# A conformer convolution on one core: output weights loaded ahead of their split, and the modulation's matmuls placed inside the channel tiles

## Chip, core and metric

The kernel runs on one core of one Trainium2 chip. The metric is the device time of one execution in microseconds (us). Before the change the median of three timed runs is 2841.52 us (2840.78 to 2841.62).

## The reference

Two layers run over 256 context tokens ("prompt", p) and 2048 latent tokens ("sample", s), of width 1024. Layer 0 is a convolution branch, layer 1 a neighbourhood attention. The change touches layer 0 alone:

```python
def conv_branch(h, w_in, dw_w, dw_b, ln_g, ln_b, w_out):
    a, b, z = jnp.split(h @ w_in, 3, axis=-1)
    u = a * jax.nn.sigmoid(b)
    u = lax.conv_general_dilated(u, dw_w[:, None, :], ...,        # 31 taps, one filter per channel
                                 feature_group_count=CONV_WIDTH) + dw_b
    u = layer_norm(u, ln_g, ln_b)
    u = jax.nn.silu(u) * jax.nn.silu(z)
    return u @ w_out
...
        shift, scale, gate = ada_params(c, ada_w[i], ada_b[i])    # silu(c) @ w + b, in three parts
        h = modulate(x, norm_g[i], shift, scale)
...
        x = x + gate[:, None] * out
```

## The kernel before

**Products.** Everything is float32. A weight or activation is split into a rounded high part and the rest (hi, lo), and a product is the sum of three matmuls: hi by hi, lo by hi, hi by lo (`project`, L351 to L353). A product of 128 channels by 512 tokens takes 8 x 3 = 24 matmuls of 128x512.

**Channel tiles.** `conv_layer` goes twice through eight channel tiles of 128 channels: first with the tokens of chunk A, then with chunk B, the two sample blocks of 512 tokens that begin at 1024 and 1536. Tiles are numbered 0 to 15 here, so tiles 8 to 15 are chunk B, and tile 15 is the last. A chunk B tile has six products, named (part, block): part 1 is the sigmoid's argument, part 0 is a, part 2 is z. The order is (1,0), (1,1), (0,0), (0,1), (2,0), (2,1), and in tile 8 (1,0), (0,0), (2,0), (1,1), (0,1), (2,1). All products of a tile, and the modulation's matmuls, take turns in two PSUM banks ("mm"), in the order in which they are issued. A bank is free when its product has been evacuated: part 1 by ACT (L449, sigmoid), part 0 by VectorE (L451, u = a * sigmoid, called the u evacuation), part 2 by ACT (L454, copy of z, which then goes to memory).

**The filter.** Each tile's 31-tap filter is cut into two halves of the token range, cv_n_0 and cv_n_1 (n is the channel tile). ACT makes scaled copies (L480) that GpSimd adds up (L483) for 11 or 12 of the taps. VectorE does the other taps as a chain of multiply-adds in two PSUM accumulators of the pool "acc" (L500, L502; L498 on ACT begins the second), and joins both sums (L506). Half 1 comes first on VectorE, then half 0, which begins from GpSimd's sum. Each tile's u evacuation (0,1) starts the chain on its own half 1. The result goes to memory (L510, `vc_d`).

**The modulation.** The vectors shift, scale and gate come from `ada_chunk`: a load of 2 MB of weights (adaw, L211), 16 matmuls of 32 output rows (ada, L216), a copy to SBUF on ACT (adam, L221), and then either a transposing matmul and an addition for a gate part (adat L225, adao L228, stored to memory L229 and read back as the `gate` rows L245) or eight small ones for shift and scale (adat L232, L239). Eight chunks are spread over the ends of tiles 8 to 15: two of layer 0's gate, six of layer 1.

**The layer norm.** `norm_stages` normalizes 128 tokens: load (L681, L683), reduction over channels (L687), mean by a matmul (L695), subtraction (L697), square (L700), variance (L706), scale as a diagonal (L709, L712) spread by a matmul (ln_rb, L715), multiplication (L719), eight Silu (L722), multiplication by silu(z) (L726), and the split of the result on GpSimd (L105, L108). Prompt tiles p0 and p128 and sample tile s0 run inside the convolution, in the buffer `ln_work`.

**The output weights.** `out_weight` loads w_out in eight pieces of 128x1024 into two buffers ("raw"), each followed by its split: co_h on ACT (L747) and co_l on VectorE (L111). The parts go into two "slot" buffers each for hi and lo, which had held other things: the first lo buffer holds the activations of block 1024, read by (2,0) of the last tile. `conv_out_pipeline` then multiplies: per 128 tokens two halves of 512 outputs, each in two quarters of 12 matmuls (co_p, co_s; L821, L822, L824), then the gate and the residual on VectorE (L830, L831).

**What sets the order.** In `conv_layer` each step is an event with a time, `at(t, f)`; the events are sorted by time, and that is the order of issue on TensorE, ACT, VectorE and GpSimd. The times are a plan in us; no instruction waits for them. The layer norm of s0, the gates and `out_weight` are written behind `conv_layer`. On VectorE, ACT and GpSimd the scheduler places them; `high_priority` moves a step as far ahead as its inputs and buffers are planned to allow. SP's loads and stores run in the queue's order, and one whose buffer is not free holds up those behind it. `conv_out_pipeline` has its own fixed order on TensorE. Its PSUM pool "lnps" lies where "acc" was, so its first layer-norm matmul (ln_s_mu of s128, L695) cannot start before VectorE's last join L506 of cv_7_0. The modulation's placing is these lines, with ADA_TIME = 3.1:

```python
        for j, (i, c) in enumerate([(0, 4), (0, 5)] + [(1, c) for c in range(6)]):
            g = self.ada_chunk(i, c)
            t = begin[NK + 1 + j] - ADA_TIME
            for dt in (-ADA_AHEAD, 0, 0.1, ADA_TIME - 0.5, ADA_TIME + ADA_LAG, ADA_TIME + ADA_LAG + 1.2)[: 6 if c < 4 else 5]:
                at(t + dt, step_of(g))
```

Of the kernel before, what the change touches and what calls it, by code (L numbers as in the profile page):

```python
# [11 lines left out]
F32 = mybir.dt.float32  # L12
# [6 lines left out]
P = 128  # L19
D = 1024  # L20
NK = D // P
# [18 lines left out]
ADA_TIME = 3.1  # L40
# [3 lines left out]
LN_TIMES = (0, 6, 14, 18, 21, 25, 33, 37, 47, 49, 52, 54, 54.1, 60, 62)  # L44
ADA_AHEAD = 4.0
ADA_LAG = 3.5
LEAD = 1.9
TMP = 4
BEGIN = 10
# [27 lines left out]
class Kern:  # L77
# [278 lines left out]
    def conv_layer(self, part_a, part_b):  # L356
# [4 lines left out]
        nc, io = self.nc, self.io  # L361
# [5 lines left out]
        begin, free = [0.0], [0.0, 0.0]  # L367
# [6 lines left out]
        for s in range(2 * NK):  # L374
# [32 lines left out]
            t = base  # L407
# [106 lines left out]
            def put(t, f, *args):  # L514
                at(t, lambda: f(*args))


            t = max(done[0], free[0])
            put(t - 0.2, scaled, 0, 0, ("sum", 0))
            for tap in range(1, npool):  # L520
                put(t + 0.6 - LEAD, scaled, 0, tap, (0, tap))
                put(t + 0.6, add, 0, tap)
                t += pool_step[0]
            ready = t + 0.8
            t = max(done[1], free[1])
# [5 lines left out]
            t = swap  # L531
# [6 lines left out]
            t = swap + 0.3  # L538
            for tap in range(npool - 1):
                put(t - LEAD, scaled, 1, tap, (1, tap))  # L540
                put(t, add, 1, tap)
# [81 lines left out]

        for j, (i, c) in enumerate([(0, 4), (0, 5)] + [(1, c) for c in range(6)]):
            g = self.ada_chunk(i, c)
            t = begin[NK + 1 + j] - ADA_TIME
            for dt in (-ADA_AHEAD, 0, 0.1, ADA_TIME - 0.5, ADA_TIME + ADA_LAG, ADA_TIME + ADA_LAG + 1.2)[: 6 if c < 4 else 5]:
                at(t + dt, step_of(g))

        for i, (load, rms, first, every, gap) in enumerate(((begin[3], begin[3] + 14, begin[3] + 26, 3.0, 30), (begin[7] + 3, begin[7] + 14, begin[8] - 7.6, 1.2, 9.6))):  # L630
            src, t0, n = part_b[i]
            for pair in range(2):
# [27 lines left out]
                t = first + gap * pair  # L660
# [75 lines left out]
            pass  # L736
        return y[0]

    def out_weight(self, w, name, res):

        nc = self.nc
        for k in range(NK):
            if k % 4 == 0:
                hi, lo = (self.slot(F32R, f"{name}_{s}{k}", [P, NK // 2, D]) for s in "hl")
            raw = self.raw(w[k * P : k * P + P, :], [P, D], f"{name}_raw{k}")
            yield
            nc.scalar.copy(hi[:, k % 4, :], raw)  # L747
            self.rest_dve(lo[:, k % 4, :], raw, hi[:, k % 4, :])
            res[0].append(hi[:, k % 4, :])
            res[1].append(lo[:, k % 4, :])  # L750
            yield

    def conv_out(self, w, blocks, ready, res=None):
# [511 lines left out]
    def phase1(self):  # L1265
        tc = self.tc
        with ExitStack() as c:
            late = c.enter_context(ExitStack())
            self.rp = late.enter_context(tc.tile_pool(name="rp", bufs=1, side="right"))
            self.sp = Tagged(c.enter_context(tc.tile_pool(name="sp", bufs=1)), {"slot": 4, "t4": 8, "raw": 2, "st": 6})  # L1270
            self.sm = c.enter_context(tc.tile_pool(name="sm", bufs=3))
            self.ps = c.enter_context(tc.tile_pool(name="ps", bufs=2, space=bass.MemoryType.PSUM))
            with tc.tile_pool(name="convp", bufs=2) as self.up, tc.tile_pool(name="acc", bufs=2, space=bass.MemoryType.PSUM) as self.pc:
                E = mybir.EngineType
                ordered = {E.PE, E.Activation, E.DVE, E.Pool}
                with tc.manual_schedule(engines=ordered):
                    self.conv_layer([("p", 0, 256), ("s", 0, 512), ("s", 512, 512)], [("s", 1024, 512), ("s", 1536, 512)])
                work = self.room[0]
                self.ready.append(self.conv_norm("s", 0, [work[:, i] for i in range(3)] + [self.t4(F32R, f"ln_s0_y{t}") for t in "hl"]))
                self.gate = [self.spread_row(self.t4(F32, f"gate0_{g}", [P, D]), self.gate_d[0, g]) for g in range(2)]  # L1280
                w = [[], []]
                for _ in self.out_weight(self.io["conv_w_out"][0], "co", w):
                    pass
            self.hp = c.enter_context(tc.tile_pool(name="hp", bufs=1))
            extra = c.enter_context(ExitStack())
            self.xp = extra.enter_context(tc.tile_pool(name="extra", bufs=1))
            norms = extra.enter_context(ExitStack())
            self.pc = norms.enter_context(tc.tile_pool(name="lnps", bufs=1, space=bass.MemoryType.PSUM))
            A, B = [], []
            rest = [("s", 768, 256), ("s", 1024, 512), ("s", 1536, 512)]  # L1290
            with tc.manual_schedule(engines={E.PE}):
                ready = self.conv_out_pipeline(w, [("p", 0, 256), ("s", 0, 512), ("s", 512, 256)], self.ready, [("s", 768), ("s", 896)], A)
            out = self.conv_out(w, rest, ready)
            self.weave(self.na_rest(A), out, 2)
            prep = itertools.chain(out, *(self.layer1_block(*b, B) for b in rest[1:]))
            self.weave(self.na_values(A, lambda: None), prep, 2)
            for _ in itertools.chain(prep, self.layer1_block(*rest[0], B)):
                pass
            late.close()
            norms.close()  # L1300
            rest = self.na_rest(B)
            with tc.tile_pool(name="bp", bufs=1, side="right") as self.bp:
                with tc.tile_pool(name="mb", bufs=1, side="right") as self.mb:
                    side = itertools.chain(self.context_keys(), self.masked_bias())
                    self.weave(self.na_values(B, lambda: next(rest)), side, 2)
                    self.weave(itertools.islice(rest, 13), side, 3.6)
                    for _ in side:
                        pass
                with tc.tile_pool(name="pq", bufs=2, side="right") as pq, tc.tile_pool(name="pqs", bufs=1, space=bass.MemoryType.PSUM) as pps:
                    side = itertools.chain(self.gated_weights(), self.context_values())  # L1310
                    side = self.mixed(self.prompt_attention(pq, pps), side, 40 / 52)
                    self.weave(itertools.islice(rest, 8), side, 11.5)
                    for _ in side:
                        pass
            extra.close()
            self.start_attention()
            for _ in rest:
                pass
# [435 lines left out]
```

## Time and profile before

| what | value |
|---|---|
| timed runs, median (least to greatest) | 2841.52 us (2840.78 to 2841.62) |
| the profiled execution, its own time | 2847.02 us |
| its span, from the first to the last instruction | 2845.2 us |
| granted TensorE clock, mean | 0.981 |
| busy in the span: TensorE, VectorE, ACT, GpSimd | 95%, 65%, 51%, 53% |
| the convolution's products of the last tile end at | 703.9 us |
| first layer-norm matmul of the output pipeline | 739.99 us |

In the profile PE is TensorE (PEld its weight loads), DVE VectorE, ACT ScalarE, POOL GpSimd, and SPq the queue of SyncE that issues the DMAs. A row of a timeline has its start and its length, then engine, line, operation, output<-input, tile and number of instructions; in brackets stands how long the engine was idle before it, and what released it. Names have lost their numbers: cv_s stands for the sums of all tiles.

### The profile page before, as it was taken

How to read it: one execution, taken by the hardware profiler on the slowest of the kernel's cores; microseconds unless marked ns; L12 is line 12 of the kernel's file. 1: busy time of each engine (PE TensorE's matmuls, PEld its weight loads, DVE VectorE, ACT ScalarE, POOL GpSimd, SP SyncE). 2: the span in 40 equal slices, each digit the busy share in tenths (PEclk: the TensorE clock that was granted, in tenths of full speed). 3: DMA queues.
4: the chain of work that ended last, by engine and by line, in shares of the span. 5: the costliest groups of instructions: out<-in, count | busy, mean ns of one | idle time of the engine just before them, and what ended most of it. 6: DMA issues, size and time to landing. Idle time of an engine off the chain costs nothing. (4 is left out here: it accounts for less than half of the span.)

```text
span 2845.2 us, 45399 instructions
## 1 busy us (share of the span) xinstructions
PE 2702.7 (95%) x16079; PEld 2339.1 (82%) x16079; DVE 1848.0 (65%) x3126; ACT 1448.6 (51%) x2544; POOL 1507.1 (53%) x1631
## 2 busy tenths in 40 slices
PE   6999999999899999999989999879999999999998
PEld 4888877777677888999988888768888898888887
DVE  4789989999886510023455632157787787777885
ACT  4457565667544311234222244246676666666774
POOL 4679878889653343355113325235555555455563
PEclk9999999999899999999999999999999999999999
DMA  7233554555445554447789996688876787866763
GB/s 254 68 121 117 185 187 158 179 177 187 154 120 164 165 156 130 131 141 229 240 285 347 346 307 194 185 247 221 245 206 190 200 216 181 239 184 178 199 168 105
DMA packets 435627, 548.02 MB, mean 193 GB/s; under 512 B 42945, under 2 KB 306201, under 8 KB 435272
## 3 DMA queue, kind: packets, MB, share of 16 engines
q1 hardware_dynamic: 430080, 522.17, 61.3%
q10 hardware_dynamic: 5320, 22.95, 2.1%
q8 instruction: 128, 2.10, 0.3%
q14 instruction: 99, 0.81, 0.1%
HBM read 359.86 MB, written 189.22 MB: 193 GB/s over the span
## 5 line engine op out<-in xcount | busy, mean ns | idle before, releaser
L1508 POOL TENSOR_SCALAR sa_p<-sa_p,sa_m 128x992 f32<-128x992 f32 (+2 forms) x256 | 278.6, 1088 | 445.7 <-DVE sa_m L1507 321.7
L502 DVE SCALAR_TENSOR_TENSOR cv<-u,dw,cv 128x640 f32<-128x640 f32 (+2 forms) x570 | 427.9, 822 | 3.7 <-ACT cv L498 2.8
L1523 ACT CAST sa_pt<-sa_T 128x512 fp32r<-128x512 f32 (+3 forms) x512 | 275.2, 588 | 235.0 <-PE sa_T L1514 230.6
L111 DVE TENSOR_TENSOR sa_pt<-sa_T,sa_pt 128x512 fp32r<-128x512 f32 (+3 forms) x512 | 328.4, 682 | 3.2 <-ACT sa_pt L1523 3.0
L351 PE MATMUL ci_ps<-h_s_hi,ci_wh 128*128 128x512 f32 x768 | 307.5, 400 | 2.0 <-DVE shift L239 1.0
L353 PE MATMUL ci_ps<-h_s_hi,ci_wl 128*128 128x512 f32 x768 | 303.2, 395 | 0.0
L352 PE MATMUL ci_ps<-h_s_lo,ci_wh 128*128 128x512 f32 x768 | 302.9, 394 | 0.0
L1500 DVE TENSOR_REDUCE sa_m<-sa_S 128x1 f32<-128x512 f32 x256 | 176.2, 688 | 184.2 <-PE sa_S L1482 169.7
L1506 ACT ACTIVATE sa_p<-sa_S,sa_m 128x992 f32<-128x992 f32 (+2 forms) x256 | 267.3, 1044 | 53.7 <-DVE sa_m L1502 42.4
L1514 PE MATMUL sa_T<-ident,sa_p 128*128 128x128 f32 (+3 forms) x2048 | 271.6, 275 | 8.1 <-DVE sa_pt L111 7.3
L1514 PEld LDWEIGHTS sa_T<-ident,sa_p 128*128 128x128 f32 (+3 forms) x2048 | 238.5, 138 | 42.5 <-issue 12.0
L480 ACT ACTIVATE cv_p<-u,dw 128x640 f32<-128x640 f32 (+2 forms) x326 | 241.4, 770 | 55.4 <-POOL cv_s L483 37.7
L483 POOL TENSOR_TENSOR cv_s<-cv_s,cv_p 128x519 f32<-128x519 f32 (+1 forms) x155 | 233.1, 1504 | 68.3 <-DVE cv_s L506 45.5
L483 POOL TENSOR_TENSOR cv_p<-cv_p,cv_p 128x520 f32<-128x520 f32 (+1 forms) x155 | 227.7, 1469 | 27.1 <-ACT cv_p L480 19.5
L1543 PE MATMUL sa_O<-sa_pt,a_v 120*128 120x256 f32 (+5 forms) x1280 | 192.5, 281 | 0.0
L1538 PE MATMUL sa_O<-sa_pt,cv 128*128 128x256 f32 x1024 | 176.3, 295 | 4.2 <-DVE 1_0_of L1557 1.7
L351 PEld LDWEIGHTS ci_ps<-h_s_hi,ci_wh 128*128 128x128 f32 x768 | 145.5, 189 | 39.3 <-ACT cv_p L480 2.5
L1502 DVE CUSTOM_DVE_ANT_0 sa_S<-sa_S,a_bm,sa_m 128x480 f32<-128x480 f32 (+2 forms) x256 | 170.9, 668 | 9.1
L353 PEld LDWEIGHTS ci_ps<-h_s_hi,ci_wl 128*128 128x128 f32 x768 | 145.1, 189 | 33.8
L352 PEld LDWEIGHTS ci_ps<-h_s_lo,ci_wh 128*128 128x128 f32 x768 | 145.6, 190 | 30.9
L1543 PEld LDWEIGHTS sa_O<-sa_pt,a_v 120*128 120x128 f32 (+2 forms) x1280 | 169.1, 193 | 0.0
L351 PE MATMUL ni_s<-h_s_hi,nis_wh 128*128 128x512 f32 x384 | 152.2, 396 | 12.4 <-DVE ni_s_l L111 8.7
(843 smaller groups left out, 7198.6 us busy)
## 6 DMA issues: line engine op xcount, KB each, us to landing
adaw<-in_ada_w SPq DMA_DIRECT2D x24, 1024.0 KB
ci_w<-in_conv_w_in SPq DMA_DIRECT2D x48, 512.0 KB
a_bm<-bm_d SPq DMA_DIRECT2D x32, 720.0 KB
x_s<-in_x_sample SPq DMA_DIRECT2D x32, 512.0 KB
vs_d<-v_s SPq DMA_DIRECT2D x128, 128.0 KB
a_qh<-qh_d SPq DMA_DIRECT2D x128, 128.0 KB
a_ql<-ql_d SPq DMA_DIRECT2D x128, 128.0 KB
o_x<-x_d SPq DMA_DIRECT2D x32, 512.0 KB
```

The lines of the kernel that those rows point to most:

```text
L111: self.nc.vector.tensor_tensor(out=lo, in0=src, in1=hi.bitcast(F32), op=ALU.subtract)
L351: self.nc.tensor.matmul(out, wh[:, k, :], hh[:, k, :], start=k == 0, stop=False)
L352: self.nc.tensor.matmul(out, wh[:, k, :], hl[:, k, :], start=False, stop=False)
L353: self.nc.tensor.matmul(out, wl[:, k, :], hh[:, k, :], start=False, stop=k == NK - 1)
L480: nc.scalar.activation(t, st["u"][:, c0 + tap : c1 + tap], AF.Copy, scale=self.dw[:, ct, tap : tap + 1])
L483: nc.gpsimd.tensor_tensor(out=st["sum", half], in0=st["sum", half], in1=st[half, tap], op=ALU.add)
L502: nc.vector.scalar_tensor_tensor(out=out, in0=u, scalar=w, in1=first, op0=ALU.mult, op1=ALU.add)
L1506: nc.scalar.activation(p[:, n], S[:, n], AF.Exp, scale=-1.0, bias=m[:, 2:3], accum_out=m[:, 3:4])
L1508: nc.gpsimd.tensor_scalar(out=p[:, n], in0=p[:, n], scalar1=m[:, 3:4], scalar2=1.0, op0=ALU.mult, op1=ALU.mult)
L1514: nc.tensor.transpose(t[:w, c * P : c * P + P], p[:, x + c * w : x + c * w + w], self.ident)
L1523: nc.scalar.copy(pt[:w, 0, part, :, at], t)
L1543: nc.tensor.matmul(dst, v[:w, c0 + c].rearrange("p s d -> p (s d)"), loc[:, lo:hi], start=False, stop=s == 1 and c == 3)
```

## The change

Two things change. Each of the modulation's eight chunks stands 12 us earlier in the table of events. And `out_weight` is started before the layer norm of s0 and the gates: it asks for seven pieces at once, 0, 1, 3 and 4 in buffers of the pool "t4", 2 in the unused fourth part of `ln_work`, 5 and 6 in "raw"; piece 7 is asked for after the split of piece 5. Both parts of the split have high priority.

```diff
+ADA_EARLY = 12.0
...
-            t = begin[NK + 1 + j] - ADA_TIME
+            t = begin[NK + 1 + j] - ADA_TIME - ADA_EARLY
...
-    def out_weight(self, w, name, res):
+    def out_weight(self, w, name, spare, res):
...
+        room = lambda k: self.t4(F32, f"{name}_raw{k}", [P, D]) if k in (0, 1, 3, 4) else self.sp.tile([P, D], F32, tag="raw", name=f"{name}_raw{k}")
+        raws = []
+
+        def load(k):
+            raws.append(spare if k == 2 else room(k))
+            nc.sync.dma_start(raws[k], w[k * P : k * P + P, :])
+
+        for k in range(NK - 1):
+            load(k)
+        yield
         for k in range(NK):
             if k % 4 == 0:
                 hi, lo = (self.slot(F32R, f"{name}_{s}{k}", [P, NK // 2, D]) for s in "hl")
-            raw = self.raw(w[k * P : k * P + P, :], [P, D], f"{name}_raw{k}")
-            yield
-            nc.scalar.copy(hi[:, k % 4, :], raw)
-            self.rest_dve(lo[:, k % 4, :], raw, hi[:, k % 4, :])
+            with self.tc.high_priority():
+                nc.scalar.copy(hi[:, k % 4, :], raws[k])
+                self.rest_dve(lo[:, k % 4, :], raws[k], hi[:, k % 4, :])
             res[0].append(hi[:, k % 4, :])
             res[1].append(lo[:, k % 4, :])
+            if k == NK - 3:
+                load(NK - 1)
             yield
...
                 work = self.room[0]
+                w = [[], []]
+                weights = self.out_weight(self.io["conv_w_out"][0], "co", work[:, 3].rearrange("p k t -> p (k t)"), w)
+                next(weights)
                 self.ready.append(self.conv_norm("s", 0, [work[:, i] for i in range(3)] + [self.t4(F32R, f"ln_s0_y{t}") for t in "hl"]))
                 self.gate = [self.spread_row(self.t4(F32, f"gate0_{g}", [P, D]), self.gate_d[0, g]) for g in range(2)]
-                w = [[], []]
-                for _ in self.out_weight(self.io["conv_w_out"][0], "co", w):
+                for _ in weights:
                     pass
```

Lines of the changed kernel stand 1 further down than before up to `out_weight`, 11 further at its casts (L758) and 13 further behind it.

TensorE at the end of the last tile, before: in the names ci_ps is a product's bank and co_p the prompt's output product.

```order
L353 MATMUL ci_ps_7_2_1_6331<-h_s_hi,ci_7_2_wl 128x512
L216 MATMUL ada_ps_5_6381<-adaw_5_6361,cs 32x512 x8
L225 MATMUL adat_ps_5_6412<-adam_5_6397,sel 2x512
L821 MATMUL co_p_0_6568<-co_h_6513,ln_y 128x512
L822 MATMUL co_p_0_6568<-co_l_6514,ln_y 128x512
```

TensorE in the last tile now, from the end of (0,1) to the beginning of (2,0); ln_s_rb is the layer norm's scale for s0:

```order
L353 MATMUL ci_ps_7_0_1_6244<-h_s_lo,ci_7_0_wh 128x512
L354 MATMUL ci_ps_7_0_1_6244<-h_s_hi,ci_7_0_wl 128x512
L217 MATMUL ada_ps_5_6281<-adaw_5_6240,cs 32x512 x8
L716 MATMUL ln_s_rb<-ln_s_dg,ones 128x128
L352 MATMUL ci_ps_7_2_0_6294<-h_s_hi,ci_7_2_wh 128x512
L353 MATMUL ci_ps_7_2_0_6294<-h_s_lo,ci_7_2_wh 128x512
```

The modulation's two parts have moved ahead of (2,0) and, for adat, ahead of (2,1); the same holds in tiles 9 to 14. In tile 8 ada stands between (1,1) and (0,1), and adat behind (0,1). Behind (2,1) of the last tile co_p now follows at once.

VectorE in the last tile before, from the u evacuation of (0,1):

```order
L451 TENSOR_TENSOR u_7_6088<-ci_ps_7_0_1_6241,u_7_6088 128x512
L500 TENSOR_SCALAR cv_7_1_0_6310<-u_7_6088,dw 128x519
L502 SCALAR_TENSOR_TENSOR cv_7_1_0_6310<-u_7_6088,dw,cv_7_1_0_6310 128x519
L502 SCALAR_TENSOR_TENSOR cv_7_1_1_6314<-u_7_6088,dw,cv_7_1_1_6314 128x519
L502 SCALAR_TENSOR_TENSOR cv_7_1_0_6310<-u_7_6088,dw,cv_7_1_0_6310 128x519
L502 SCALAR_TENSOR_TENSOR cv_7_1_1_6314<-u_7_6088,dw,cv_7_1_1_6314 128x519
L687 TENSOR_REDUCE ln_s_s_6621<-ln_s_v 128x128
L502 SCALAR_TENSOR_TENSOR cv_7_1_0_6310<-u_7_6088,dw,cv_7_1_0_6310 128x519
L111 TENSOR_TENSOR co_l_6514<-co_raw_6515,co_h_6513 128x1024
L111 TENSOR_TENSOR co_l_6514<-co_raw_6519,co_h_6513 128x1024
```

VectorE at the same place now, a few rows in (the first two rows are the filter's, the piece of the first split lies in ln_work):

```order
L503 SCALAR_TENSOR_TENSOR cv_7_1_1_6326<-u_7_6096,dw,cv_7_1_1_6326 128x519
L720 TENSOR_TENSOR ln_work<-ln_work,ln_s_rb 128x1024
L503 SCALAR_TENSOR_TENSOR cv_7_1_0_6322<-u_7_6096,dw,cv_7_1_0_6322 128x519
L503 SCALAR_TENSOR_TENSOR cv_7_1_1_6326<-u_7_6096,dw,cv_7_1_1_6326 128x519
L503 SCALAR_TENSOR_TENSOR cv_7_1_0_6322<-u_7_6096,dw,cv_7_1_0_6322 128x519
L112 TENSOR_TENSOR co_l_6527<-ln_work,co_h_6526 128x1024
L112 TENSOR_TENSOR co_l_6527<-co_raw_6480,co_h_6526 128x1024
L112 TENSOR_TENSOR co_l_6527<-co_raw_6475,co_h_6526 128x1024
L112 TENSOR_TENSOR co_l_6527<-co_raw_6477,co_h_6526 128x1024
L229 TENSOR_TENSOR adao_5_6347<-adat_ps_5_6345,adao_5_6347 2x512
```

Four splits now stand together ahead of adao, three more follow nine filter rows later, and the last stands between the filter rows of cv_7_0. The layer norm's L720 and L727, which stood in the filter of cv_6_0 before, have moved behind the u evacuation. The reduction of s128 (L688) has moved from here to just ahead of the join of cv_7_1. On GpSimd the split of s0's result (L106, L109) has moved from the adds of cv_6_1 into those of cv_7_0.

## Prediction

> **What bounds the kernel now.** I read the page first, then the busy time by stretches of the span, then the timelines of TensorE and VectorE where TensorE stands idle.
>
> ```profile
> span 2845.2 us, 45399 instructions
> PE 2702.7 (95%) x16079; PEld 2339.1 (82%) x16079; DVE 1848.0 (65%) x3126; ACT 1448.6 (51%) x2544; POOL 1507.1 (53%) x1631
> ```
>
> TensorE is busy for 95% of the span, so a change gains only where TensorE waits. The busy time by stretches (PE, PEld, DVE, ACT, POOL, then the granted clock, DMA share, GB/s) shows the largest hole at the change's place.
>
> ```profile
> 700.00:720.00 20.00, 12.75 (x50) 6.55 (x48) 20.00 (x23) 12.13 (x17) 17.26 (x11) 0.91 0.58 191
> 720.00:740.00 20.00, 12.71 (x34) 8.58 (x34) 18.55 (x26) 11.03 (x14) 17.83 (x11) 0.66 0.34 108
> 740.00:760.00 20.00, 20.00 (x93) 16.62 (x94) 14.49 (x19) 7.28 (x14) 4.56 (x7) 1.00 0.74 253
> ```
>
> From 700 to 740 TensorE lacks 7.25 + 7.29 = 14.54 us, while VectorE is busy for 38.55 of 40. TensorE's rows there (start, length, line, idle before):
>
> ```profile
> 692.44 0.39 PE L353 MATMUL ci_ps<-h_s_hi,ci_wl 128*128 128x512 f32 x1
> ...
> 703.50 0.40 PE L353 MATMUL ci_ps<-h_s_hi,ci_wl 128*128 128x512 f32 x1
> 703.83 1.92 PE L216 MATMUL ada_ps<-adaw,cs 128*32 128x512 f32 x16
> 711.09 1.86 PE L225 MATMUL adat_ps<-adam,sel 128*2 128x512 f32 x2 [5.34 <-ACT adam L221]
> ...
> 728.84 0.80 PE L822 MATMUL co_p<-co_l,ln_y 128*128 128x512 f32 x1 [1.06 <-DVE co_l L111]
> ...
> 731.14 0.63 PE L821 MATMUL co_p<-co_h,ln_y 128*128 128x512 f32 x1
> ...
> 739.99 0.49 PE L695 MATMUL ln_s_mu<-ln_s_s,ones 128*128 128x128 f32 x2 [1.45 <-DVE cv_s L506]
> ```
>
> The first row ends the last u product; the convolution's products end at 703.50, the last modulation piece follows, and the output product then waits for one weight piece after another. At 739.99 the first layer-norm matmul starts. Its PSUM pool is opened over the filter's accumulators, so it waits for VectorE's last join. VectorE, from the evacuation of that u product (zero of "relative" below) to this join:
>
> ```profile
> 692.94 0.69 DVE L451 TENSOR_TENSOR u<-ci_ps,u 128x512 f32<-128x512 f32 x1
> ...
> 697.04 2.09 DVE L502 SCALAR_TENSOR_TENSOR cv<-u,dw,cv 128x519 f32<-128x519 f32 x3 [1.81 <-ACT cv L498]
> ...
> 724.24 2.08 DVE L111 TENSOR_TENSOR co_l<-co_raw,co_h 128x1024 fp32r<-128x1024 f32 x1 [0.87 <-ACT co_h L747]
> ...
> 738.58 0.69 DVE L830 TENSOR_TENSOR co_op<-co_p,gate 128x512 f32<-128x512 f32 x1 [0.58 <-PE co_p L824]
> 739.19 0.75 DVE L506 SCALAR_TENSOR_TENSOR cv_s<-cv,more,cv_s 128x520 f32<-128x520 f32 x1
> ```
>
> From 692.94 to that matmul at 739.99 are 47.05 us, of them 1.81 + 0.87 + 0.58 = 3.26 idle, so 43.79 of work (0.1 of it the handover). Until 740 the bound is VectorE's list, not the weights: TensorE's hole is the time in which that list outlasts the convolution's products. After 740 TensorE runs without a gap in either order, so the end moves by what this matmul moves.
>
> **The change, part by part: the tail.** The split of the eight pieces (L111) stays behind the last u evacuation on VectorE, since its first output takes the buffer that the product (2,0) reads. So none of the 43.79 us leaves this stretch. Two operations enter it: the layer norm's multiplications (L719, L726) ran earlier before, and now stand behind the evacuation, because their scale's matmul stands behind the moved modulation.
>
> ```profile
> 677.62 1.20 DVE L719 TENSOR_TENSOR ln_work<-ln_work,ln_s_rb 128x1024 f32<-128x1024 f32 x1
> 678.75 4.08 DVE L502 SCALAR_TENSOR_TENSOR cv<-u,dw,cv 128x520 f32<-128x520 f32 x6
> 682.98 1.23 DVE L726 TENSOR_TENSOR ln_work<-ln_work 128x1024 f32<-128x1024 f32 x1 [0.15 <-ACT ln_work L722]
> 684.12 4.09 DVE L502 SCALAR_TENSOR_TENSOR cv<-u,dw,cv 128x520 f32<-128x520 f32 x6
> ```
>
> Their steps, to the row behind, are 1.13 and 1.14: together 2.27, and the work becomes 46.06. Then the idle time. Ahead of the first split VectorE has seven filter rows at 4.08/6 = 0.68 and one L719, 5.9 us in all. The product (2,0) starts behind the modulation (1.92) and a small matmul, at about 695.0, and ends 24 matmuls later (half of 703.50 − 692.44, 5.5 us) at 700.5, relative 7.5. The idle is 1.6, with the old wait for ACT L498 inside it. It could be 0 to 3.
>
> The second idle is at the filter chain that continues GpSimd's sum of cv_7_0:
>
> ```profile
> 686.89 1.07 POOL L105 TENSOR_SCALAR ln_s_yh<-ln_work 128x1024 fp32r<-128x1024 f32 x1
> ...
> 689.20 2.40 POOL L108 TENSOR_TENSOR ln_s_yl<-ln_work,ln_s_yh 128x1024 fp32r<-128x1024 f32 x1
> ...
> 698.39 18.69 POOL L483 TENSOR_TENSOR cv_p<-cv_p,cv_p 128x520 f32<-128x520 f32 x11
> ```
>
> ACT's rows of the same step, in the order before:
>
> ```profile
> 678.46 1.28 ACT L722 ACT_TABLE_LOAD   x1
> 679.75 3.19 ACT L722 ACTIVATE ln_work<-ln_work,more 128x128 f32<-128x128 f32 x8
> ```
>
> And the splits and casts as groups (shortest, median, longest ns):
>
> ```profile
> L111 DVE TENSOR_TENSOR co_l<-co_raw,co_h x8: 1206/1430/2321, 701.7 to 727.6; 128x1024 fp32r<-128x1024 f32 x8
> L747 ACT CAST co_h<-co_raw x8: 1028/1046/1048, 691.6 to 725.9; 128x1024 fp32r<-128x1024 f32 x8
> ```
>
> L105 and L108 now stand among the eleven adds, each add 18.69/11 = 1.70. ACT has four casts of 1.05, the table load and Silu (1.28 + 3.19) and three more casts ahead of a copy of z and the next scaled tap, which so comes at about relative 16. From there GpSimd has that add, L105, L108 and seven adds, about 17.1, and ends near 33. VectorE gets there at relative 31.4: 7.5, then seven splits at 1.5 and adao at 0.6 (11.1), L726 (1.14), thirteen filter rows (8.8), the reduction (2.0, as the row of 569.06 below) and the join (0.7). The second idle is 1.6, between 0 and 4.
>
> In sum 46.06 + 1.6 + 1.6 = 49.3, against 47.05 before: +2.2. The splits have the widest price: I take 1.5 each, a little over the group's median of 1.43; eight at its least (1.21) give −2.5, at 2.0, toward its greatest (2.32), +4. I keep 1.5, since GpSimd adds through nearly all of the stretch in either order. TensorE waits in it again: for the product (2,1), whose PSUM bank VectorE's adao frees behind four splits, at relative 14.5, some 6 us in place of the 5.34. The last split is ready at relative 37.9 (31.4 + 1.6, five filter rows, one split), against 728.84 − 692.94 = 35.9, and the output product's rest, 738.58 − 728.84 = 9.7, ends at 47.6 with a residual and the join behind it: also no earlier.
>
> [...]
>
> **The middle tiles.** With the modulation's two parts between products of the tile, TensorE takes a bank sooner after VectorE's u evacuation is due. TensorE's ends of two products and VectorE's evacuations in tiles 8, 9 and 12:
>
> ```profile
> 438.67 0.39 PE L353 MATMUL ci_ps<-h_s_hi,ci_wl 128*128 128x512 f32 x1
> ...
> 444.27 0.40 PE L353 MATMUL ci_ps<-h_s_hi,ci_wl 128*128 128x512 f32 x1
> ...
> 581.93 0.39 PE L353 MATMUL ci_ps<-h_s_hi,ci_wl 128*128 128x512 f32 x1
> ```
>
> ```profile
> 443.17 0.69 DVE L451 TENSOR_TENSOR u<-ci_ps,u 128x512 f32<-128x512 f32 x1
> ...
> 464.52 0.69 DVE L451 TENSOR_TENSOR u<-ci_ps,u 128x512 f32<-128x512 f32 x1 [1.08 <-PE ci_ps L353]
> ...
> 586.83 0.68 DVE L451 TENSOR_TENSOR u<-ci_ps,u 128x512 f32<-128x512 f32 x1
> ```
>
> And around tile 12's beginning, TensorE's wait behind adat, VectorE's wait for a load, and SP's issues before it:
>
> ```profile
> 561.67 0.95 PE L232 MATMUL adat_ps<-sel,adam 128*128 128x2 f32 x8
> 563.63 0.50 PE L351 MATMUL ci_ps<-h_s_hi,ci_wh 128*128 128x512 f32 x1 [1.01 <-DVE shift L239]
> 569.06 2.04 DVE L687 TENSOR_REDUCE ln_p_s<-ln_work 128x128 f32<-128x1024 f32 x1 [5.49 <-DMA ln_work<-vc_d]
> 556.22 0.93 SPq L211 DMA_DIRECT2D adaw<-in_ada_w  x2
> ...
> 561.51 0.36 SPq L681 DMA_DIRECT2D ln_work<-vc_d  x1
> ```
>
> In tile 8 the u product ends at 439.06 and (2,1) at 444.67; with the modulation's 1.92 and about 0.95 around it, (2,1) could start at 441.9, but its bank is free only at 443.86: +2.0. VectorE waits for TensorE at 464.52 (tile 9), so the slip is passed on. In tile 12 the evacuation is 4.5 us behind its product (582.32 to 586.83), which a product covers today; with 1.92 in its place it would cost up to 587.51 − 582.32 − 1.92 = 3.3. That lateness follows the 5.49 at 569.06, a load issued at 561.51 behind the two modulation loads at 556.22. Those are now asked for some 12 us earlier, so I expect the load sooner and take 0. The wait of 1.01 behind adat goes, since a product now stands there: −1.0. Sum +1.0, from −1.4 to +5.3.
>
> **The early loads** cost nothing in this sum. They stand on SP ahead of the filter's stores, two of them behind a wait for the last tile's product (1,1).
>
> ```profile
> 693.53 5.25 SPq L510 DMA_DIRECT2D vc_d<-cv_s  x2
> ```
>
> That product ends two products, 11 us, before 692.83, and the stores' time comes later still. They gain nothing either: what was late was the split's place. The result is +1.0 + 2.2 = +3.2. The profiled execution took 2847.02 us, its span and 1.8 around it, and would take 2850.2; the timed runs' median of 2841.52 lies 5.5 below it, and 2844.7 is the forecast for it.
>
> **The rivals.** A, faster: the hole closes, since TensorE finds all pieces split. Removing its 14.54 us gives 2827. For it speaks that the waits after 712 name the split, as at 728.84; against it, that VectorE's list is no shorter and TensorE's row at 739.99 waits for its end. It decides if the filter rows run at well under 0.68. B, slower: the u evacuation holds the banks. +2.0 in tile 8, +3.3 in tile 12 and +2.2 in the tail, without the −1.0, make +7.5, 2849.0. It decides where the evacuation starts over 1.92 − 0.69 = 1.2 us behind its product; tile 8 shows it, tile 12 only if the load stays late. C, the change doesn't do what it says: priority cannot pull the split ahead of (2,0) and the moved modulation meets no wait; then 2841.5. D, warm clock: the rows from 731.14 take 0.63 instead of the 0.39 of 703.50, after idle time. If a shorter hole keeps the clock up, eight such rows give back 8 x 0.24, about 2 us: 2842.7, if VectorE follows. [...]
>
> **How the numbers follow.** The forecast has 0.5, A 0.12, B 0.2, C 0.13, D 0.05. A measurement here tells 0.2% or 5.7 us from no change: under 2835.8 is faster, over 2847.2 slower. The forecast's own bounds are, below, −1.4 + 2.2 − 2.5 − 3.2 (no idle) = −4.9 and, above, +3.2 + 4 + 1.7 = +8.9, with splits at 2.0 and half of tile 12's price. Forecast, C and D fall within, but for 0.04 of the forecast on the upper side and 0.02 on the lower: faster 0.14, same 0.62, slower 0.24. The range goes from 2836 (−4.9, rounded) to 2851 (B with splits 2 us dearer): it leaves out A and some hundredths above.
>
> **What would show it.** Right: L452 of tile 8 releasing TensorE; L720 and L727 behind the last u evacuation; TensorE waiting for adao about 6 us; the matmul ln_s_mu within 2 us of 49.3 behind that evacuation. Wrong: TensorE's idle between 700 and 740 under 8 us, or ln_s_mu still waiting for VectorE although the list ended earlier than 45 us, or waits of over 2 us for L452 in tiles 12 to 14.

## The result, and the profile after

The changed kernel takes 2857.77 us (median of 5 runs, 2854.3 to 2864.64), the kernel before beside it 2840.78 (5 runs, 2833.67 to 2841.62): 17.0 us more, a ratio of 1.0059 with a 95% interval of 1.0045 to 1.0073. Forecast were 2844.7 and a range of 2836 to 2851. The change is slower, and the range didn't hold the time.

The page shows an unchanged sum of work, and TensorE still at 95%:

```profile
span 2853.2 us, 45418 instructions
...
PE 2698.9 (95%) x16079; PEld 2336.5 (82%) x16079; DVE 1848.1 (65%) x3126; ACT 1443.3 (51%) x2542; POOL 1503.0 (53%) x1631
```

The spans, 2845.2 and 2853.2, differ by 8 only, since single executions spread: from the second mean matmul of the output pipeline to the end, which the change doesn't touch, the kernels of this study took 2082 to 2093 us (before 2093, after 2085). The places are therefore compared inside the stretch that the change touches: from ACT's sigmoid of product (1,1) of tile 8 to the second mean matmul. Of before and of after (start, length, line, idle before):

```profile
433.50 0.60 ACT L449 ACTIVATE u<-ci_ps 128x512 f32<-128x512 f32 x1 [2.12 <-PE ci_ps L353]
...
751.78 0.38 PE L695 MATMUL ln_s_mu<-ln_s_s,ones 128*128 128x128 f32 x2
```

```profile
433.76 0.60 ACT L450 ACTIVATE u<-ci_ps 128x512 f32<-128x512 f32 x1 [2.11 <-PE ci_ps L354]
...
705.96 0.69 DVE L452 TENSOR_TENSOR u<-ci_ps,u 128x512 f32<-128x512 f32 x1 [0.59 <-PE ci_ps L354]
...
755.23 0.59 PE L696 MATMUL ln_s_mu<-ln_s_s,ones 128*128 128x128 f32 x2 [2.11 <-DVE cv_s L507]
...
768.60 0.38 PE L696 MATMUL ln_s_mu<-ln_s_s,ones 128*128 128x128 f32 x2
```

318.28 us became 334.84, or +16.6, nearly all of the 17.0. Its parts: the last u evacuation moved from 692.94 to 705.96 (**middle tiles, +13.0**); from it to the first mean matmul 49.27 in place of 47.05 (**tail, +2.2**); from the first mean matmul to the second 13.37 in place of 11.79 (**behind the join, +1.6**). Of these 16.8, 0.3 were there at the sigmoid already, ahead of the change.

**Middle tiles.** The waits of TensorE between 400 and 760 (engine and line, releaser: us in total, times, longest), of after:

```profile
PE ci_ps L352 <- DVE u L452: 9.8, 5, 4.4
...
PE ci_ps L352 <- DVE adao L229: 4.8, 1, 4.8
...
PE ci_ps L352 <- ACT z L455: 1.2, 1, 1.2
PE ci_ps L352 <- ACT adam L222: 0.7, 1, 0.7
```

Before, no product waited for a u evacuation; its waits for a bank in the same stretch are these:

```profile
PE ci_ps L351 <- DVE shift L239: 1.0, 1, 1.0
PE ci_ps L351 <- DVE gs L239: 0.4, 1, 0.4
```

The changed kernel's five waits for L452 stand in tiles 8, 11, 12, 13 and 14. TensorE at tile 12's:

```profile
586.16 0.39 PE L354 MATMUL ci_ps<-h_s_hi,ci_wl 128*128 128x512 f32 x1
586.48 1.92 PE L217 MATMUL ada_ps<-adaw,cs 128*32 128x512 f32 x16
592.79 0.76 PE L352 MATMUL ci_ps<-h_s_hi,ci_wh 128*128 128x512 f32 x1 [4.39 <-DVE u L452]
593.35 0.63 PE L353 MATMUL ci_ps<-h_s_lo,ci_wh 128*128 128x512 f32 x1
...
598.05 0.59 PE L352 MATMUL ci_ps<-h_s_hi,ci_wh 128*128 128x512 f32 x1
598.47 0.41 PE L353 MATMUL ci_ps<-h_s_lo,ci_wh 128*128 128x512 f32 x1
```

The product ends at 586.55; the modulation's 16 matmuls take 1.92; then the next product needs the bank of the one before, whose evacuation VectorE starts only at 591.96. Behind the wait the matmuls start 0.43 apart instead of 0.23, some thirteen of them: half the clock (0.50 granted from 591.6 to 598.4), another 2.6 us. In tile 8 a wait of 1.85 has eight such matmuls behind it (1.6 us); the waits of 1.65, 1.03 and 0.84 have none. All waits of tiles 8 to 14 come to 11.7 (9.8 + 1.2 + 0.7), before to 1.4 (1.0 and 0.4, both for L239), so +10.3; the slow matmuls to 4.2 less the 1.6 that stood behind before's wait of 1.01, so +2.6. Together 12.9.

VectorE ahead of that evacuation:

```profile
572.15 2.03 DVE L688 TENSOR_REDUCE ln_p_s<-ln_work 128x128 f32<-128x1024 f32 x1 [2.22 <-DMA ln_work<-vc_d]
576.26 1.80 DVE L503 SCALAR_TENSOR_TENSOR cv<-u,dw,cv_p 128x520 f32<-128x520 f32 x1 [2.08 <-POOL cv_p L484]
...
591.96 0.68 DVE L452 TENSOR_TENSOR u<-ci_ps,u 128x512 f32<-128x512 f32 x1
```

VectorE's wait for the load is 2.22 instead of 5.49, but the load did not land sooner: it landed at 572.15, 3.1 us later than before (569.06), and the wait is shorter because VectorE reached this row 6.4 us later. SP's waits between 550 and 570 name what held the load. The first row is of before, the second of after, and the third is the load's issue in after:

```profile
SPq L681 <- POOL ln_y L108: 2.9, 1, 2.9
```

```profile
SPq L682 <- POOL ln_y L109: 2.7, 1, 2.7
```

```profile
567.96 0.36 SPq L682 DMA_DIRECT2D ln_work<-vc_d  x1
```

In both kernels the load is issued right behind the split of the earlier prompt tile on GpSimd, which frees `ln_work`: at 561.51 behind a split that ends at 561.48, and now at 567.96 behind one that ends at 567.93. From the issue to the landing it took 4.19 us instead of 7.55, with the modulation's two loads 6.5 us further ahead (549.68 for 556.22), but the issue itself came 6.5 later, as GpSimd did. The next row waits another 2.08 for GpSimd's sum, which is as late. In tile 11 VectorE, which GpSimd follows by way of ACT, was already 6.0 behind before's times (its (0,1) u evacuation at 549.83 for 543.85). So in tile 12 the evacuation is 5.4 us behind its product (586.55 to 591.96), more than the 4.5 of before.

**Tail.** The busy time by stretches, and VectorE's rows:

```profile
700.00:720.00 20.00, 15.20 (x72) 10.06 (x71) 17.86 (x23) 15.80 (x24) 9.71 (x8) 0.95 0.09 33
720.00:740.00 20.00, 12.39 (x42) 9.02 (x40) 19.87 (x21) 9.45 (x16) 18.15 (x11) 0.76 0.76 236
740.00:760.00 20.00, 14.59 (x45) 11.09 (x46) 18.22 (x24) 9.84 (x14) 14.42 (x11) 0.70 0.28 88
```

```profile
708.82 1.21 DVE L720 TENSOR_TENSOR ln_work<-ln_work,ln_s_rb 128x1024 f32<-128x1024 f32 x1
...
713.48 1.82 DVE L112 TENSOR_TENSOR co_l<-ln_work,co_h 128x1024 fp32r<-128x1024 f32 x1 [1.44 <-PE ci_ps L353]
715.22 3.48 DVE L112 TENSOR_TENSOR co_l<-co_raw,co_h 128x1024 fp32r<-128x1024 f32 x3
...
720.56 1.21 DVE L727 TENSOR_TENSOR ln_work<-ln_work 128x1024 f32<-128x1024 f32 x1
...
727.68 6.74 DVE L112 TENSOR_TENSOR co_l<-co_raw,co_h 128x1024 fp32r<-128x1024 f32 x3
...
741.81 2.23 DVE L112 TENSOR_TENSOR co_l<-co_raw,co_h 128x1024 fp32r<-128x1024 f32 x1
```

L720 and L727 stand behind the last u evacuation, TensorE waits 4.8 for adao, and the last split is ready at 744.04, relative 38.1 (forecast: some 6, and 37.9). VectorE is busy for 55.95 of the 60 us. TensorE's hole did not close: it lacks 4.8, 7.6 and 5.4 in the three rows.

### The profile page after: what moved, and what is told of

It reads as the page before. It is cut to its first block, busy times and chain, and to the rows that moved or that the text cites. A ratio compares the mean times of both kernels' runs of the same rounds, so it can differ in the third digit from the quotient of the medians.

```text
span 2853.2 us, 45418 instructions
## 1 busy us (share of the span) xinstructions
PE 2698.9 (95%) x16079; PEld 2336.5 (82%) x16079; DVE 1848.1 (65%) x3126; ACT 1443.3 (51%) x2542; POOL 1503.0 (53%) x1631
## 4 chain that ended last, share of the span: by engine, by line
PE 74%; DMA 9%; DVE 7%; POOL 3%; ACT 3%; issue 2%; SPq 2%; POOLq 0%; ACTq 0%; DVEq 0%
PE sa_T L1529 7%; PE ni_s L352 5%; PE ni_s L353 5%; PE ni_s L354 5%; PE ci_ps L352 5%; PE ci_ps L353 5%; PE ci_ps L354 5%; PE sa_O L1558 5%; PE sa_O L1553 4%; PE sa_S L1497 3%; PE sa_S L1496 3%; DVE cv L503 3%; PE o L1659 2%; PE o L1661 2%; PE o L1660 2%
## 5 line engine op out<-in xcount | busy, mean ns | idle before, releaser
L1529 PEld LDWEIGHTS sa_T<-ident,sa_p 128*128 128x128 f32 (+3 forms) x2048 | 239.1, 138 | 41.1 <-issue 10.3
```

The source lines that it names most:

```text
L1529: nc.tensor.transpose(t[:w, c * P : c * P + P], p[:, x + c * w : x + c * w + w], self.ident)
```

## The experiments

They are told in the order of the questions; the times of before are those measured beside each. A table of all stands at the end.

**Which part of the change costs?** `x1_weights_only` and `x2_modulation_only` take one part each.

```diff
-ADA_EARLY = 12.0
+ADA_EARLY = 0.0        # x1, in the changed kernel; x2 is the kernel before with the 12.0
```

> The early loads and the split's priority alone; the modulation stands where it stood. Theory (the modulation's parts take PSUM banks too early in tiles 8 to 14, and the tail is VectorE's list): the middle goes back to that of before, no wait of TensorE for the u evacuation; in the tail L719 and L726 are ahead of the u evacuation again, the first layer-norm matmul comes about 47 us behind it, although the last split is ready some 6 us sooner than before. Time within 4 us of before. Rival (the early loads and the priority themselves cost the time, by SP's queue or by splits that displace the filter): 10 us or more slower. Second rival (TensorE's hole is bound by the pieces): 6 to 10 us faster.

> The modulation 12 us earlier alone; the weights are loaded and split as before. Theory: the whole of the middle's +13 us, with waits for the u evacuation of 10 us in sum and half-clock stretches behind the longest, and +1 to +3 in the tail by L719 and L726; 14 to 17 us slower than before. Rival (early loads or priority carry the loss): within 5 us of before.

x1 took 2841.33 against 2839.84 (ratio 1.001, 0.9996 to 1.0024), x2 2856.46 (1.0059, 1.0041 to 1.0076). The modulation's place carries the whole loss; x2 has the changed kernel's waits for the u evacuation, and longer ones for the weight pieces; its tail is 50.9, +3.8 where +1 to +3 was expected:

```profile
PE ci_ps L352 <- DVE u L452: 9.7, 5, 4.4
PE co_p L823 <- DVE co_l L112: 9.3, 5, 2.9
PE co_p L822 <- ACT co_h L748: 9.0, 3, 4.2
```

x1 answers what the early weights bring. All eight pieces are split and multiplied by 732.75, 39.1 us behind the last u evacuation (before 45.6), and then TensorE stands:

```profile
741.69 0.77 PE L696 MATMUL ln_s_mu<-ln_s_s,ones 128*128 128x128 f32 x2 [8.94 <-DVE cv_s L507]
```

So all that the pieces gain goes into one wait for VectorE's last join: the weights were not the bound. The list did not get shorter either: VectorE waits for 0.7 us instead of 3.3, but its eight splits take 15.7 instead of 12.7.

**Is it the bank?** `x3_own_banks` gives the moved modulation of tiles 8 to 13 the other pair of banks.

```diff
+        tag = "mm" if (i, c) in ((1, 4), (1, 5)) else "tr"
...
-        pm = self.pc.tile([P, 1024], F32, tag="acc", name=f"ada_ps{i}_{c}")[:, :512] if early else self.mm_bank(f"ada_ps{i}_{c}")
+        pm = self.pc.tile([P, 1024], F32, tag="acc", name=f"ada_ps{i}_{c}")[:, :512] if early else self.mm_bank(f"ada_ps{i}_{c}", tag)
...
-        pt = self.mm_bank(f"adat_ps{i}_{c}", "tr" if early else "mm")
+        pt = self.mm_bank(f"adat_ps{i}_{c}", tag)
```

> The changed kernel, but six of the eight modulation chunks (tiles 8 to 13) use the other two PSUM banks, those of transposes and of the layer norm, so the products keep their turn of two banks. Theory: waits for the u evacuation in tiles 8 to 13 and their half-clock stretches go, only tile 14's 1.7 us stays; 2 to 5 us slower than before, 10 to 13 us faster than the changed kernel. Rival (VectorE's lateness itself, from the moved steps on ACT and GpSimd, is what costs; TensorE waits for it in the next product anyway): 10 us or more slower than before.

The waits for the u evacuation in tiles 8 to 12 and the slow matmuls behind them are gone (the granted clock is 1.00 from 450 to 600), but the time is 2853.72 (1.0047, 1.0031 to 1.0063), 13.9 above before: far from the expectation and within the rival's 10 or more. The layer norm of s0 uses the other pair too, and its matmuls now stand elsewhere in the order; TensorE waits at new places:

```profile
PE ci_ps L353 <- DVE u L453: 3.3, 1, 3.3
PE ci_ps L353 <- ACT z L456: 2.6, 1, 2.6
PE ada_ps L218 <- DVE ln_s_rs L711: 2.0, 1, 2.0
PE ci_ps L353 <- ACT u L451: 1.5, 1, 1.5
PE adat_ps L234 <- ACT adam L223: 1.5, 1, 1.5
```

The waits for the bank in those tiles are shown to be just that; the total is not explained by them alone.

**Is it the distance?** `x4_modulation_6us` is the kernel before with ADA_EARLY at 6.0, which puts the two parts around another product.

> The modulation alone, 6 us earlier in place of 12: one product earlier, so that product (2,0) stands between the u product and the modulation's matmul, which then takes the u product's bank. Theory (what counts is a product's 5.5 us of cover): no wait for the u evacuation over 1 us, small waits for copies of z; the tail as before; within 5 us of before. Rival (any earlier place costs in proportion to the shift): half of the loss, 6 to 9 us slower than before.

2846.16 (1.0019, 1.0007 to 1.0031), 6.3 above before: in the rival's range, though the interval (2.0 to 8.8 us) reaches the theory's 5. Up to the last u evacuation it loses 9.3 us of the changed kernel's 12.8; its tail is 44.25, 2.8 shorter than before's. The waits went to ACT's copy of z in tiles 10 and 11 (5.1 in two), and 3.0 for the u evacuation remain in tile 8.

**Is the evacuation too late?** `x5_early_u` and its control `x6_before_early_u` issue the u evacuations of tiles 8 to 15 some 3 us earlier, in the changed kernel and in the one before:

```diff
-                at(first[-1][0] + 0.1 - START if first else t - 1.5, evacuate)
+                at(first[-1][0] + 0.1 - START if first else t - (4.5 if part == 0 and chunk else 1.5), evacuate)
```

> The changed kernel, with the u evacuations of tiles 8 to 15 issued 3 us earlier in the event table (VectorE meets them some four filter rows sooner); banks, modulation and weights as changed. Theory (the modulation between products lets TensorE ask for a bank before VectorE's late u evacuation has freed it): the waits for L452, 9.8 us in 5, fall to under 3, the half-clock stretches behind tiles 8 and 12 go, and the last u evacuation comes 6 to 10 us sooner than the 13 us it had lost; the time is 2847 to 2851 against 2857.8 of the changed kernel and about 2840 before. Rival (the modulation's matmuls cost this by themselves between products, or VectorE, now waiting for the product, loses what TensorE gains): the waits move to other releasers and the time stays at 2854 or above.

> The kernel before, with the same earlier u evacuations, as the control of x5. Theory: before, no product waits for L452, so nothing is there to win; the time is within 3 us of before. Rival (an earlier u evacuation is a gain of its own, whatever the modulation does, so x5 tells nothing of the banks): 5 us or more faster than before.

x5: 2854.17 against 2838.59 (1.0061, 1.0046 to 1.0077); x6: 2851.46 (1.0051, 1.0034 to 1.0068). The waits of x5, then of x6:

```profile
PE ln_s_mu L696 <- DVE cv_s L507: 13.0, 1, 13.0
...
PE ci_ps L352 <- ACT z L455: 5.1, 3, 2.6
PE co_p L835 <- DVE co_l L112: 4.5, 2, 4.1
...
PE ci_ps L352 <- DVE u L452: 0.8, 1, 0.8
```

```profile
PE co_p L822 <- DVE co_l L111: 10.8, 5, 3.2
PE co_p L821 <- ACT co_h L747: 10.6, 3, 4.8
```

In x5 the wait for the u evacuation falls from 9.8 to 0.8, as the theory says, but the last u evacuation comes only 3.4 us sooner than after's (702.61), where 6 to 10 were expected, and the time is the rival's. Three waits for z copies come in its place, with slow matmuls behind the two longest of them (1.91 and 2.56; 0.63 long in place of 0.39), and the tail is 51.0 long. The control shows why this is no repair: the same step costs the kernel before 12.9 us, of them 8.0 in the tail (55.0 in place of 47.05, its weight pieces waited for eight times), where I had expected nothing. There the list is not what the first mean matmul waits for: VectorE's last join ends at 744.95, and the output product, which waits for its pieces, runs on until 751.1. I read it so that the order on VectorE is tight on both sides, and that an evacuation further ahead delays the filter and the splits behind it; no run shows this apart from the rest.

**Do the parts add?** `x10_last_tile_only` moves the modulation in tile 15 alone.

```diff
-            t = begin[NK + 1 + j] - ADA_TIME - ADA_EARLY
+            t = begin[NK + 1 + j] - ADA_TIME - ADA_EARLY * (j == 7)
```

> The changed kernel with the modulation's parts early in tile 15 alone; tiles 8 to 14 have them at the tiles' ends again, as before. Theory (the loss is made of separate parts: 13.0 us in tiles 8 to 14, 2.2 in VectorE's list of the last tile, 1.6 of half clock behind the last join): the first part goes, so the stretch from tile 8 to the second mean matmul is 3 to 5 us longer than before, and the time 3 to 5 us above it, with no wait of over 1.1 us for L452. Rival (the order in the last tile makes the loss, or the parts hang together): 8 us or more above before.

2847.16 against 2840.33 (1.0022, 1.0012 to 1.0032). Only 0.2 us of waits for the u evacuation are left, and the stretch is 2.9 longer than before. The median is 6.8 above, more than the stretch tells: the profiled execution, 2841.46, is the second shortest of the twelve. The median's interval (3.4 to 9.1 us) reaches both the expectation and the rival's 8. Of the 17 us about 8 or more went with tiles 8 to 14.

**Is VectorE's list the bound of the tail?** `x8_fewer_taps` is x1 without eight taps of the last tile's half 0, so part of the filter is missing; `x7_splits_on_gpsimd` is x1 with two of the splits on GpSimd.

```diff
-            for k, tap in enumerate(range(npool, TAPS)):
-                put(t - ACT_FIRST * (k == 1), dve, 0, k, tap, k == last_odd(TAPS - npool))
+            for k, tap in enumerate(range(npool, TAPS - 8 * (s == 15))):      # x8
+                put(t - ACT_FIRST * (k == 1), dve, 0, k, tap, k == last_odd(TAPS - npool - 8 * (s == 15)))
...
-                self.rest_dve(lo[:, k % 4, :], raws[k], hi[:, k % 4, :])
+                (self.rest_pool if k in (4, 5) else self.rest_dve)(lo[:, k % 4, :], raws[k], hi[:, k % 4, :])      # x7
```

> The weights alone (as x1), with 8 of the taps of the last tile's half 0 left out on VectorE (that part of the filter is not computed). Theory (VectorE's list is the bound): the list is 8 x 0.68 = 5.4 us shorter, the first layer-norm matmul comes 42 to 43.5 us behind the last u evacuation instead of 48.05, its wait for L507 is 3 to 4.5 instead of 8.94, and the time is 4 to 6 us under x1's 2841.3. Rival (the weight pieces or TensorE's own work are the bound): matmul and time stay within 1.5 us of x1.

> The weights alone (as x1), with the splits of pieces 4 and 5 on GpSimd (2.40 us each there) instead of VectorE (about 1.64 each). Theory (until the first layer-norm matmul the bound is VectorE's list): the list is 3.3 us shorter, TensorE's wait for L507 of 8.94 us shrinks to about 6, and the time is about 2838, 3 us under x1's 2841.3. Rival (GpSimd's sum of cv_7_0, whose 4.58 us of idle time the two splits use up, or contention at the splits becomes the bound): VectorE waits for GpSimd ahead of cv_7_0 by 2 us or more and the time is 2841 or above.

In x8 the last u evacuation is at 692.32 and the first mean matmul follows 42.7 us behind it, in place of 48.05 in x1, as expected:

```profile
734.99 0.77 PE L696 MATMUL ln_s_mu<-ln_s_s,ones 128*128 128x128 f32 x2 [4.21 <-DVE cv_s L507]
```

The list sets that matmul. The time, 2838.02 against 2838.59 (1.0, 0.9987 to 1.0013), is some 2 to 3 us under x1's, less than the 5.4 left out and than the 4 to 6 expected; its stretch, in the table below, is 4.5 shorter than x1's. x7 came out at the rival's time, 2841.96 (1.0019, 1.0006 to 1.0032), with the matmul 49.05 behind the evacuation, though VectorE's wait for GpSimd's sum is 1.18 and not the 2 that the rival named. Its VectorE rows:

```profile
716.88 1.23 DVE L112 TENSOR_TENSOR co_l<-co_raw,co_h 128x1024 fp32r<-128x1024 f32 x1 [0.94 <-ACT co_h L758]
719.29 1.79 DVE L503 SCALAR_TENSOR_TENSOR cv<-u,dw,cv_p 128x520 f32<-128x520 f32 x1 [1.18 <-POOL cv_p L484]
...
722.92 1.24 DVE L844 TENSOR_TENSOR x_p<-x_p,co_op 128x512 f32<-128x512 f32 x1
...
729.62 1.77 DVE L844 TENSOR_TENSOR x_p<-x_p,co_op 128x512 f32<-128x512 f32 x1
```

VectorE's splits take 12.0 us in place of x1's 15.7, but two waits (0.94 and 1.18) came in, the row behind GpSimd's sum takes 1.79 in place of 0.75, and the residuals L844, 0.68 and 0.69 in x1, take 1.24 and 1.77, though GpSimd adds beside them in both kernels. The work moved to GpSimd came back as waits and slower rows.

**Can the early weights be made to pay?** TensorE's wait for the join in x1 exists only because the layer norm's banks lie over the filter's accumulators. `x9_norm_banks` (x1) and the control `x11_before_norm_banks` (before) place s128's three small results elsewhere.

```diff
-        bank = lambda t: self.mm_bank(nm + t, "tr") if room else self.pc.tile([P, 512], F32, tag="ln", name=nm + t, bufs=2)
+        bank = lambda t: self.mm_bank(nm + t, "tr") if room or nm == "ln_s128" else self.pc.tile([P, 512], F32, tag="ln", name=nm + t, bufs=2)
```

> The weights alone (as x1), and the three small layer-norm results of s128 (mean, variance, scale) in the banks "tr" instead of the pool that is opened over the filter's accumulators. Theory (in x1 the weights' gain is real, 8.94 us of finished pieces, but the first layer-norm matmul waits for VectorE's last join only because of where its bank lies): that wait goes, the 7.2 us of output product that stand between the mean and the variance matmul run in the hole, and the variance, which still needs a square in the old pool, then waits for the join and some 3 us of square and reduction. The second mean matmul comes 4 to 5 us sooner than in x1, and the time is 2835 to 2839, 1 to 5 us below the kernel before. Rival (the hole only moves to the variance matmul, with half-clock matmuls behind it, or VectorE's list grows by the subtraction that now stands in it): within 1.5 us of x1.

> The kernel before, with the banks of x9, as its control. Theory: there TensorE waits only 1.45 us for the last join, since the output product's last pieces are as late as the list; the time is 0 to 2 us below before. Rival (the banks are a gain without the early weights): 4 us or more below before.

x9 took 2843.17 against 2840.33 (1.0008, 0.9996 to 1.002): the mean matmul runs at 730.41 without waiting, and the hole moves to the variance, whose square still lies in the old pool:

```profile
743.84 0.58 PE L707 MATMUL ln_s_var<-ones,ln_s_s 128*128 128x2 f32 x2 [7.55 <-DVE ln_s_s L688]
...
744.86 0.63 PE L835 MATMUL co_p<-co_l,ln_y 128*128 128x512 f32 x1
```

That is the rival. x11 took 2838.26 (0.999, 0.9976 to 1.0004), 2.1 below before, at the edge of its expectation and not told from before. No kernel here is shown to beat the kernel before.

The table sets each kernel's stretch (sigmoid of tile 8 to the second mean matmul, against 318.28) beside its median against before's. Its second column is the first part of the stretch, up to the last u evacuation (against 259.44):

| kernel | to the last u evacuation, us | whole stretch, us | median, us |
|---|---|---|---|
| after | +12.8 | +16.6 | +17.0 |
| x1 weights only | +0.9 | +3.3 | +1.5 |
| x2 modulation only | +12.7 | +16.4 | +16.6 |
| x3 own banks | +9.8 | +13.2 | +13.9 |
| x4 modulation 6 us earlier | +9.3 | +6.5 | +6.3 |
| x5 after, early u | +9.1 | +15.6 | +15.6 |
| x6 before, early u | +4.5 | +12.4 | +12.9 |
| x7 splits on GpSimd | +0.8 | +4.2 | +3.4 |
| x8 fewer taps | +0.9 | -1.2 | -0.6 |
| x9 weights, norm banks | +0.9 | +2.8 | +2.8 |
| x10 last tile only | -1.2 | +2.9 | +6.8 |
| x11 before, norm banks | +0.9 | -0.9 | -2.1 |

Apart from x10, stretch and median agree within 2 us: what these kernels change in time, they change inside this stretch. The kernels that leave the middle tiles as they were (x1, x7, x8, x9, x11) all lie 0.8 to 0.9 above before's profiled execution up to the last u evacuation, so a difference of 1 us there tells nothing.

## Why the prediction was wrong

**The tail's total was right, and partly by luck.** It is 49.27 against 49.3, with L720 and L727 in the list and the wait for adao. Its reason, that VectorE's list and not the weights bounds the tail, is what x1 and x8 show. Rival A falls with them: in x1 TensorE does find the pieces split, and gains nothing. But two terms were off and cancelled. The splits come to 14.27, 1.6 more than the 12.71 of before; VectorE's idle time was 1.4 in place of the forecast 3.2, since the second idle, 1.6 at GpSimd's sum of cv_7_0, did not come. "GpSimd adds through nearly all of the stretch in either order" does not hold: GpSimd was idle for 4.1 us from 708.8 and for 7.2 from 714.2. The splits' spread goes with it here: 1.16 each while GpSimd stands idle (715.22), 2.25 while it adds (727.68). L720 and L727 met it mostly idle and took 1.21 each, as before.

**The early loads** cost little, as I said: x1's 1.5 us median is not told from nothing.

**The failed step** is the one on the middle tiles: "Those are now asked for some 12 us earlier, so I expect the load sooner and take 0", and with it "Sum +1.0, from −1.4 to +5.3". It was +13.0. The load landed 3.1 us later, because what had held it before was GpSimd's split of the earlier tile (2.9 us of SP's waiting) and not the modulation's two loads ahead of it, and that split came 6.5 us later; GpSimd's sum was as late. I had taken the order of SP's rows for the cause of the stall and had not looked at what SP itself waited for. So the evacuation fell 5.4 us behind its product, and the price that I had put at nothing was paid in full: "waits of over 2 us for L452 in tiles 12 to 14" was named as a sign of being wrong, and it came. Tile 12 cost 4.39 where its upper price was 3.3, and tiles 10, 11, 13 and 14, which I had not priced, 0.7, 1.0 + 1.2, 0.8 and 1.65. Only tile 8 (1.85 for 2.0) was as worked out.

**The half clock was left out.** I saw 0.63 rows in the tail and made a rival of them there, but gave no wait in the middle such a price: behind tiles 8 and 12 they cost 4.2 (1.6 stood there before). Rival D's warmer clock did not come: 0.76 and 0.70 were granted in the rows of 720 and 740, against 0.66 and 1.00. The sentence that "the end moves by what this matmul moves" fails for the same reason: the join's wait of 2.11, too, is followed by slow matmuls (0.63 long in place of 0.39, from 756.04 on), +1.6.

**Rival B was the mechanism**, with its condition right (an evacuation over 1.2 us behind its product, where only a modulation part covers it) and its 7.5 less than half of the 16.8. That B belongs in tiles 13 and 14 too could have been worked out from before's rows. There the evacuation starts 3.2 and 4.2 us behind the product (619.04 to 622.28, 655.75 to 659.95), which by tile 12's sum gives 2.0 and 3.0, where 0.84 and 1.65 came. In tiles 9 to 11 it is 0.0 to 0.6 behind, under B's condition; the 2.1 of tile 11 came with the change.

**Still open:** why the modulation between products costs 9 to 13 us up to the last u evacuation in all four experiments that kept it there (x2 to x5), with another late releaser in nearly each (u evacuation, z copy, adam, the layer norm). Taking the waits for the u evacuation away (x3 in tiles 8 to 13, x5) gave back only some 3 of the 12.8. That two banks with one short cover are the common cause is argued, not shown; a kernel with a third bank was not tried.

## What to carry to other kernels

Where products take turns in two PSUM banks, a short matmul group put between two of them shortens the time in which the evacuation may be late: from a product's 5.5 us to the group's own 1.9 here. Price that in every place that the loop repeats, with the evacuation's lateness from the trace, and add the slow matmuls where the trace has them behind a wait (2.6 us behind the 4.39 here, none behind the 1.65). And ask before making weights arrive earlier whether the engine that splits them has any time left: here it was busy for 38.55 of 40 us, and finished pieces only moved TensorE's wait to the end of the list. When a load is late, look at what its queue waited for before you blame the loads ahead of it.

## What the runs showed of the hardware

In the changed kernel a TensorE wait of 4.39 us is followed by some thirteen matmuls of 128x512 at 0.43 us instead of 0.23, one of 1.85 by eight, while 1.65, 1.20 and 1.03 have none behind them; a wait of 1.01, right behind narrow matmuls, had eight in the kernel before. The granted clock agrees: in the changed kernel it is 0.50 from 444.9, behind the 1.85, to 448.3 (3.4 us) and from 591.6, inside the 4.39, to 598.4 (6.8 us). In the kernel before it is 0.50 from 564.2 to 567.6, behind the 1.01, again 3.4 us. The halving behind 1.85 and 1.01, and its absence behind 1.65, is not told by the length of the wait alone; what decides it stays open.

A VectorE subtraction of 128x1024 with both inputs in SBUF took 1.16 us in the mean of three with GpSimd idle, and 2.25 in the mean of three with GpSimd adding. GpSimd's rows at the two places, of after:

```profile
721.37 1.56 POOL L484 TENSOR_TENSOR cv_p<-cv_p,cv_p 128x520 f32<-128x520 f32 x1 [7.15 <-ACT cv_p L481]
...
727.53 10.77 POOL L484 TENSOR_TENSOR cv_p<-cv_p,cv_p 128x520 f32<-128x520 f32 x6
```

In the kernel before, three of these subtractions took 1.21 us each (711.06, 720.16 and 727.58) while GpSimd was adding for 1.14 to 1.21 of them. That it adds does not alone give their length; what does was not shown.
